# Branch B's transpositions and products spread over the tile, values two tiles behind the scores, and the third head's projections ahead of the token sums

## The chip, the core and the metric

One core of one Trainium2 chip. The time is the device time of one execution in microseconds (us), the median of several runs; the profile is of one more execution of the same program. Engines: PE does matmuls (and loads their weights, PEld), DVE is the vector engine, ACT the scalar engine, POOL is GpSimd, and SP issues nearly all DMAs. PSUM is the memory that PE writes to, in banks of 128 x 512 fp32; everything else lies in SBUF or in DRAM.

## The reference

A pre-norm encoder block on 1024 tokens of width 1024, with 16 meta tokens put in front (L = 1040). Two attention branches read the same normed input h; a SwiGLU feed-forward part follows.

```python
proj = h @ w_in                       # qa ka va | qb kb vb | ga gb
# A: 4 heads of 2 x 64 (q, k) and 128 (v), every token sees every token
attn = softmax(s1) - lam * softmax(s2)     # s = q k / 8 - slope * |dist|
y_a = rms_norm(attn @ va, subln) * (1 - lambda_init)
# B: 8 query heads of 64 in 2 groups, one key/value head per group;
# a block of 128 queries sees 16 meta tokens and three blocks of 128 keys
p = exp(s - m); y_b = (p / (sum(p) + exp(sink - m))) @ vb
merged = sigmoid(ga) * (y_a @ w_ba) + sigmoid(gb) * (y_b @ w_bb)
x = x + merged @ w_o
x = x + (silu(n @ w_gate) * (n @ w_up)) @ w_down     # n = rms_norm(x)
```

## The kernel before

All matmuls have fp32 accuracy. An operand is split in a high part and a low part (hi, lo), and a product is three matmuls: hi x hi, hi x lo, lo x hi. A split is two instructions: ACT copies to the high part, and DVE or POOL subtracts it from the source for the low part. So nearly every tile that PE writes, and every weight that it reads, goes through ACT and then DVE or POOL.

**Stages.** In order, with the microseconds of the profiled execution: norm and transposition of x and the first projections (to 73); branch B (73 to 232); token sums (232 to 286); products of a Strassen-like scheme that reads them, for the queries of A and six gates (286 to 366, `product_t`); branch A (366 to 676); then the output products and the feed-forward part, which the change doesn't touch.

**Projection steps.** `project_steps` makes a projection of 128 columns in chunks of tokens; one step is the three matmuls of one 128-row block of the contraction, so a chunk has eight steps, and at its end the result is evicted and sent to DRAM (`va_evac`, `k_consume`). The chunks are 384, 384 and 272 tokens wide for keys and values of A, 512 for gates and for the second group's queries of B. Weights are loaded (`w_c`), then split by ACT (L185) and POOL (L188) in `prep`, `W_BUFS` = 2 projections ahead.

**The order.** A scheduler orders the instructions of ACT, DVE, POOL and SP from a model of the time line. PE's order, from L585 (branch B) to the end of the products and again in branch A (L878 on), is the order in which the Python code issues matmuls. Generators hold the pieces of work, and strings of slots say which one gives its next piece.

**Branch B** has 16 tiles: two groups with eight blocks of queries each. `attend_b` (L315) is one tile. For each of the four query heads it makes a pair of score matmuls into a bank (tag "bs" of PSUM, two banks), and DVE adds the distance term, takes the running maximum and writes the scores to the tile `bs` (L332); then ACT makes four exponentials (L338), DVE the denominators, and POOL normalises the four rows (L344) and copies the 16 meta columns to `bmd` (L348). `values()` does the rest of the tile: for each of its three blocks of keys (two at the ends) and then the meta block, four transpositions into a bank (tag "bt", two banks, L364), ACT's copy (L366), DVE's low part (L368), and, when more than two transposed blocks stand in the list `trs`, the products of the oldest into the bank "by" (L358: two matmuls of 512 columns for a block of keys, one for the meta block). The last product is the meta block's. ACT and DVE add the two halves of the bank (L379, L380), and four DMAs store it.

The scores of the tiles 0 and 1 are made first, in the prologue. In the loop from L592 the tile n gives scores while tile n-1 gives values, seven projection steps in a tile, by

```python
SLOTS_B = "sgsgsgstgtgttgtttgt"    # s scores of n, t values of n-1, g a projection step
```

The steps come from `fill_b` (L566): 176 in all, for values and keys of the heads 0, 1 and 2 of A, with the second group's queries of B in four pieces between those of head 0. Before the loop `B_FIRST` = 8 steps are made and one more beside each of the six pieces of tile 0's values, after it `B_LAST` = 10 and six beside the last tile's. With 14 rounds of seven, 128 steps lie in branch B, and the 48 of the third head (h = 2) lie behind it.

**Token sums.** `token_sums` (L613) makes on DVE, for a quarter of the tokens, four sums of the high and low parts of hT (L620), four more sums and differences of those (L623 to L626), and splits of the results into `tops` (L627; L121 on ACT, L122 on DVE). It is called before steps 0, 8, 16 and 24 of the third head's 48 (L636). The products (`product_t`, matmuls L696) read `tops` for four of their seven terms.

**Branch A** has 32 tiles (four heads with eight blocks). For a tile `scores_a` makes six pairs of score matmuls (L791; DVE L794), an exponential per map (L799, ACT), a scaling (L802, POOL) and the combination of both maps (L805, DVE); `transpose_a` transposes nine blocks in three banks (L817, then L820 and L821 on ACT and DVE); `values_a` makes the products of two tiles at a time (L830), and after every fourth tile `normed_a` normalises the head's output. In the loop from L888 the tile n gives scores and tile n-2 its transpositions. The slots "g" fill in projection steps of the fourth head of A and of ten gates (`fill_steps`, L737), the slots "n" step the products of older tiles (`step_tail`). At a new head `load_a` (L761) fetches its queries, keys and values from DRAM into buffers that the last head's scores still read; there `fill(G_HEAD)`, ten steps, stands ahead of the tile's slots, and 33 (`G_FIRST`) at the first head. `HOLD` = 36 of the gate steps are kept for the tail, where the products of the last tiles are made with three steps after each piece (L918 to L921).

Of the kernel before, what the change touches and what calls it, by code (L numbers as in the profile page):

```python
# [20 lines left out]
P = 128  # L21
# [9 lines left out]
BG = 2  # L31
# [11 lines left out]
SLOTS = "stgstgstgsngsnsn"  # L43
SLOTS_LAST = "stgstgstsngsnsn"
N_MORE = 13
SLOTS_B = "sgsgsgstgtgttgtttgt"
S_BUFS = (2, 2)
AT_BUFS = 2
G_BUFS = 3
HOLD = 36  # L50
PAIRS = 3
HEADS_EARLY = 3
GT_BUFS = 4
WB_BUFS = 5
G_HEAD = 10
G_FIRST = 33

QK_BUFS = 3
# [1 line left out]
X_BUFS = 2  # L60
T_LAG = 2
V_AT = 2
B_FIRST = 8
B_LAST = 10
E_STEPS = 1
OP_BUFS = 8
RING_RAW = 5
# [12 lines left out]
def encoder_block(ctx: ExitStack, tc: tile.TileContext, x, meta, norm_mix, w_in, lq1, lk1, lq2, lk2,  # L80
# [190 lines left out]
    def flush_v():  # L271
        for g in turning_v:
            for _ in g:
                pass
# [2 lines left out]
    bpool, close_bpool = pool("bpool")  # L277
    kb = [bpool.tile([P, 2, NT, 144], F32R, name=f"kb{g}") for g in range(BG)]
    vb = [bpool.tile([P, 9, P], F32R, name=f"vb{g}") for g in range(BG)]
    mds = [bpool.tile([P, 4, P], F32, name=f"bmd{i}") for i in range(2)]  # L280
    for i in range(2):
        nc.gpsimd.memset(f32(vb[i])[:, 8, :], 0.0)
        nc.gpsimd.memset(mds[i], 0.0)

    def kb_consume(st, at, n):
        b0, nb = at // P, n // P
# [28 lines left out]
    def attend_b(g, t, finish):  # L315
        nm = f"{g}_{t}"
        b0, b1 = max(t - 1, 0), min(t + 2, NT)
        nb = b1 - b0
        W = nb * 144
        j0 = b0 - t + 1  # L320
        tb = tbx[:, j0:j0 + nb, :].rearrange("p j k -> p (j k)")
        st = bpool.tile([P, 4, 432], F32, tag="bs", name=f"bs_{nm}", bufs=2)
        mn = small.tile([P, 4], F32, tag="bmn", name=f"bmn_{nm}")
        dn = small.tile([P, 4], F32, tag="bdn", name=f"bdn_{nm}")
        es = small.tile([P, 4], F32, tag="bes", name=f"bes_{nm}")
        hs = slice(4 * g, 4 * g + 4)
        for r in range(4):
            ps = bank(psum1, "bs", f"bps_{nm}_{r}", 2)
            for v in range(2):
                nc.tensor.matmul(ps[:, :W], qb[:, r, t * P:(t + 1) * P],  # L330
                                 kb[g][:, v, b0:b1, :].rearrange("p b k -> p (b k)"), start=(v == 0), stop=(v == 1))
            nc.vector.tensor_tensor_reduce(st[:, r, :W], ps[:, :W], tb, 2.0 ** -(4 * g + r + 1), nsink[:, 4 * g + r:4 * g + r + 1],  # L332
                                           ALU.add, ALU.min, mn[:, r:r + 1])
            if r < 3:
                yield
        nc.vector.tensor_tensor(es, mn, sinkb[:, hs], ALU.add)
        for r in range(4):
            nc.scalar.activation(st[:, r, :W], st[:, r, :W], AF.Exp, bias=mn[:, r:r + 1], scale=-1.0,  # L338
                                 accum_out=dn[:, r:r + 1])
        nc.scalar.activation(es, es, AF.Exp)  # L340
        nc.vector.tensor_tensor(dn, dn, es, ALU.add)
        nc.vector.reciprocal(dn, dn)
        for r in range(4):
            nc.gpsimd.tensor_scalar(st[:, r, :W], st[:, r, :W], dn[:, r:r + 1], 1.0, ALU.mult, ALU.mult)  # L344

        md = mds[t % 2]
        own = (t - b0) * 144 + P
        nc.gpsimd.tensor_copy(md[:, :, 0:2 * NM].rearrange("p r (a k) -> p r a k", a=2),  # L348
                              st[:, :, own:own + NM].unsqueeze(2).broadcast_to([P, 4, 2, NM]))

        def values():
            py = bank(psum1, "by", f"bpy_{nm}", 1)
            blocks = [(k, P, (k - b0) * 144) for k in range(b0, b1)] + [(8, P, (t - b0) * 144 + P)]
            trs = []

            def products(k, kp, tr):
                for hl in range(2 if k < 8 else 1):
                    nc.tensor.matmul(py, vb[g][:kp, k, :], tr[:kp, hl].rearrange("p r t -> p (r t)"),  # L358
                                     start=(k == b0 and hl == 0), stop=(k == 8))

            for k, kp, o in blocks:
                pt = bank(psum1, "bt", f"bpt_{nm}_{k}", 2).rearrange("p (r t) -> p r t", r=4)
                for r in range(4):
                    nc.tensor.transpose(pt[:kp, r, :], st[:, r, o:o + P] if k < 8 else md[:, r], ident)  # L364
                tr = bpool.tile([P, 2, 4, P], F32R, tag="btr", name=f"btr_{nm}_{k}", bufs=4)
                nc.scalar.activation(tr[:kp, 0], pt[:kp], AF.Copy)  # L366
                lo = tr[:, 1] if k < 8 else tr[:NM, 0]
                nc.vector.tensor_tensor(lo, pt[:lo.shape[0]], f32(tr[:lo.shape[0], 0]), ALU.subtract)  # L368
                trs.append((k, kp, tr))
                yield  # L370
                if len(trs) > 2:
                    products(*trs.pop(0))
                    yield
            while len(trs) > 1:
                products(*trs.pop(0))
                yield
            products(*trs.pop(0))
            y1 = bpool.tile([64, 512], F32, tag="by1", name=f"by1_{nm}", bufs=2)
            nc.scalar.copy(y1, py[64:128])  # L379
            nc.vector.tensor_tensor(y1, py[0:64], y1, ALU.add)  # L380
            for jj in range(2):
                for par in range(2):
                    r = 2 * jj + par
                    nc.sync.dma_start(yb_d[2 * g + jj][64 * par:64 * par + 64, t * P:(t + 1) * P],
                                      y1[:, r * P:(r + 1) * P])
            yield
        finish.append(values())
# [18 lines left out]
    def norm_x(t):  # L406
        parts = P if t < NT else NM
        i = len(done)
        done.append(t)
        p, tag, bufs = (stage, "vt", 1) if i % 3 == 2 else (bpool, "bs", 2)  # L410
        xns[t] = normed(p, xts.pop(t)[:parts], parts, gmix, f"a{t}", tag=tag, bufs=bufs)

    def turn_x(t):
# [146 lines left out]
    def v_steps_a(h):  # L560
        return v_steps(C_VA + h * P, f"va{h}", va_evac(h))
# [4 lines left out]
    def fill_b():  # L566
        def prepared(steps):
            ensure(1)
            yield from with_turns(steps)
            ensure(W_BUFS - 1)  # L570

        for h in range(HEADS_EARLY):
            yield from prepared(v_steps_a(h))
            if not h:
                for jj in range(2):
                    yield from prepared(qb_steps(1, qb, jj, Q_CHUNKS[:1]))
            yield from prepared(k_steps_a(h))
            if not h:
                for jj in range(2):
                    yield from prepared(qb_steps(1, qb, jj, Q_CHUNKS[1:]))  # L580


    order_pe = tc.manual_schedule(engines={mybir.EngineType.PE})
    order_pe.__enter__()
    more = fill_b()  # L585
    for _ in range(B_FIRST):
        next(more)
    for _ in finish.pop(0):
        next(more)
    for n in range(2, BG * NT):  # L590
        scoring, values = attend_b(*divmod(n, NT), finish), finish.pop(0)
        for what in SLOTS_B:  # L592
            next({"s": scoring, "t": values, "g": more}[what], None)
        for _ in chain(scoring, values):
            pass
    for _ in range(B_LAST):
        next(more)
    for _ in finish.pop(0):
        next(more)
    close_bpool()  # L600


# [30 lines left out]
        return (hT_hi, hT_lo)[b][:, 4 * kh + c, th * 512:th * 512 + 512]  # L633


    for i, _ in enumerate(more):  # L636
        if i % 8 == 0 and i < 32:
            token_sums(i // 8)
    flush_v()
    close_psum1()  # L640
    psum_t, close_psum_t = pool("psum_t", space=PSUM)
    psum1 = psum_t
# [217 lines left out]
    def fill(n):  # L860
        while n > 0 and n_gates[0] > 0:
            n, n_gates[0] = n - 1, n_gates[0] - 1
            next(gates, None)
# [24 lines left out]
    for n in range(AH * NT + T_LAG):  # L888
        scoring, turning = iter(()), iter(())
        if n < AH * NT:  # L890
            h, t = divmod(n, NT)
            if t == 0:
                ld = load_a(h)
                fill(G_HEAD if h else G_FIRST)
            if t % 2 == 0:
                at_ = apool.tile([P, 9, 2, 256], F32R, tag="at", name=f"at{h}_{t}", bufs=AT_BUFS)
            s = [None, None]
            tiles.append((h, t, s, at_, ld[2]))
            scoring = scores_a(h, t, ld, s)
        if n >= T_LAG:  # L900
            turning = turn(tiles[n - T_LAG])
        for what in SLOTS if n < N_MORE else SLOTS_LAST:
            if what == "s":
                next(scoring, None)
            elif what == "t":
                next(turning, None)
            elif what == "n":
                step_tail()
            else:
                fill(1)  # L910
        for _ in scoring:
            pass
        for _ in turning:
            pass
        if n >= T_LAG and tiles[n - T_LAG][1] % 2:
            tail.append(later(tiles[n - T_LAG]))
    n_gates[0] += HOLD
# [610 lines left out]
```

## Time and profile before

| | |
|---|---|
| runs | 1501.68 us median of 3 (1497.37 to 1503.5) |
| profiled execution | 1496.41 us |
| its span in the trace | 1494.5 us |
| granted clock of PE, mean | 0.993 |
| DMA | 193.13 MB, mean 129 GB/s |

The span runs from the first to the last record; the profiled execution's own time is 1.9 us longer. Busy time is the union of an engine's instructions. A row of the timeline gives start, duration, engine, line of the kernel, instruction, output <- inputs and shape; a number in brackets at its end is the time for which the engine stood idle before it, with what ended the wait. A row of the waits gives the waiting instruction, the one that released it, the sum of the waits in us, their count and the longest. Names have their buffer numbers left out: `bpt` is a bank for the transpositions of B, `btr` the transposed tile with both parts, `bpy` the bank of its products; `aps`, `apt` and `apy` are the same for A, `ak` its keys, `as` its scores; `pp_va`, `pp_ka`, `pp_qb`, `pp_g` are banks of projections. A clock share of 1.00 is the full granted clock of PE.

### The profile page before, as it was taken

Reading aid. Unit: us, or ns where it says so; the run is one execution under the profiler, and the core shown is the slowest. Engines: PE = TensorE matmul, PEld = TensorE weight load, DVE = VectorE, ACT = ScalarE, POOL = GpSimd, SP = SyncE. Lnnn points to the kernel's source line nnn. Section 1 sums busy time; section 2 is a strip of 40 time slices with the busy share of each in tenths; the row PEclk is TensorE's granted clock in tenths of the full one; section 3 lists DMA queues with packets and bytes.
Section 4 is the critical chain, followed back from the end, with each engine's and each line's share of the span. In section 5 each row is a group of like instructions: output and inputs, shape, how many; then the busy total and the mean of one; then the engine's idle time right before and its main releaser. Section 6 shows DMA issues by size and latency. Waiting matters only on the chain.

```text
span 1494.5 us, 21017 instructions
## 1 busy us (share of the span) xinstructions
PE 1446.2 (97%) x7315; PEld 1229.3 (82%) x7315; DVE 896.1 (60%) x1635; ACT 689.9 (46%) x1296; POOL 563.0 (38%) x555
## 2 busy tenths in 40 slices
PE   8999998899899999999999999999999999999997
PEld 7977788688789888978888878888888888888886
DVE  6467768721668787814442586745555554778567
ACT  6366663432555565625532463333333333444444
POOL 4244431544222322313763315544554553000344
PEclk9999999999999999999999999999999999999999
DMA  8423314433633414137653244333333333864433
GB/s 233 90 81 98 99 44 146 124 124 114 181 94 99 142 65 128 51 124 244 210 189 113 77 128 155 110 102 106 106 106 106 106 106 106 300 230 133 133 122 141
DMA packets 154203, 193.13 MB, mean 129 GB/s; under 512 B 16288, under 2 KB 98656, under 8 KB 154096
## 3 DMA queue, kind: packets, MB, share of 16 engines
q1 hardware_dynamic: 154096, 191.78, 40.6%
q8 instruction: 58, 0.95, 0.3%
q14 instruction: 49, 0.40, 0.1%
HBM read 131.24 MB, written 53.94 MB: 124 GB/s over the span
## 4 chain that ended last, share of the span: by engine, by line
PE 74%; DVE 7%; DMA 6%; issue 5%; POOL 3%; ACT 3%; SPq 1%; POOLq 0%; DVEq 0%; ACTq 0%
PE pg L1309 27%; PE pd L1403 8%; PE po L1075 6%; PE pt L696 5%; PE pp_g L215 5%; PE ppa L734 4%; PE aps L791 3%; PE apy L830 3%; POOL oa L122 3%; PE pp_qb L215 2%; DMA ak<-ka_d 2%; PE apt L817 2%; PE bpy L358 1%; PE pp_ka L215 1%; PE pp_va L215 1%
## 5 line engine op out<-in xcount | busy, mean ns | idle before, releaser
L1309 PE MATMUL pg<-t,wop 128*128 128x512 f32 x1056 | 243.0, 389 | 1.6 <-DVE wop L122 1.6
L1309 PEld LDWEIGHTS pg<-t,wop 128*128 128x128 f32 x1056 | 198.0, 188 | 43.4 <-DVE wop L122 2.0
L122 POOL TENSOR_TENSOR wop<-wf,wop 128x512 fp32r<-128x512 f32 x118 | 157.5, 1336 | 156.5 <-ACT wop L121 145.5
L1403 PE MATMUL pd<-ob,oa 128*128 128x512 f32 x924 | 210.0, 389 | 0.4 <-POOL oa L122 0.4
L1403 PEld LDWEIGHTS pd<-ob,oa 128*128 128x128 f32 x924 | 173.3, 188 | 37.0 <-POOL oa L122 0.8
L1309 PE MATMUL pg<-b,wop 128*128 128x512 f32 x792 | 183.2, 389 | 0.0
L1309 PEld LDWEIGHTS pg<-b,wop 128*128 128x128 f32 x792 | 148.5, 188 | 30.8
L121 ACT ACTIVATE wop<-wf 128x512 fp32r<-128x512 f32 x128 | 80.3, 632 | 82.3 <-PE pg L1309 50.4
L122 POOL TENSOR_TENSOR oa<-ra,oa 128x512 fp32r<-128x512 f32 x33 | 44.0, 1335 | 170.1 <-ACT oa L121 168.7
L799 ACT ACTIVATE as<-as,amn 128x1040 f32<-128x1040 f32 x64 | 74.5, 1164 | 64.9 <-DVE amn L794 50.8
L121 ACT ACTIVATE oa<-ra 128x512 fp32r<-128x512 f32 x77 | 48.7, 632 | 106.6 <-PE pd L1403 50.2
L791 PE MATMUL aps<-ak,aq 128*128 128x352 f32 (+1 forms) x384 | 92.4, 332 | 3.4 <-DMA ak<-ka_d 2.8
L188 POOL TENSOR_TENSOR wl_c<-w_c,wh_c 128x512 fp32r<-128x512 f32 x48 | 61.9, 1311 | 84.7 <-ACT wh_c L185 74.6
L1075 PE MATMUL po<-woh,mT 128*128 128x512 f32 x384 | 88.6, 390 | 0.0
L1075 PEld LDWEIGHTS po<-woh,mT 128*128 128x128 f32 x384 | 71.7, 188 | 14.7
L1133 DVE TENSOR_TENSOR s<-wf,wf 128x512 f32<-128x512 f32 x22 | 18.2, 829 | 108.1 <-DMA wf<-in_w_ff_up_dram 53.1
L791 PEld LDWEIGHTS aps<-ak,aq 128*128 128x128 f32 x384 | 66.8, 191 | 15.7 <-issue 4.4
L122 POOL TENSOR_TENSOR wop_t<-wt,wop_t 128x512 fp32r<-128x512 f32 x30 | 46.5, 1554 | 60.8 <-ACT wop_t L121 59.3
L802 POOL TENSOR_SCALAR as<-as,adn,neglam 128x1040 f32<-128x1040 f32 x32 | 38.8, 1213 | 80.6 <-DVE adn L800 71.7
L215 PE MATMUL pp_g<-hT_hi,wh_c 128*128 128x512 f32 x160 | 68.9, 431 | 0.0
L344 POOL TENSOR_SCALAR bs<-bs,bdn 128x432 f32<-128x432 f32 (+1 forms) x64 | 36.9, 596 | 75.3 <-ACT btr L366 55.7
L215 PE MATMUL pp_g<-hT_hi,wl_c 128*128 128x512 f32 x160 | 63.3, 395 | 0.0
(279 smaller groups left out, 3175.2 us busy)
## 6 DMA issues: line engine op xcount, KB each, us to landing
ra<-aop SPq DMA_DIRECT2D x77, 256.0 KB, 2.6
w_c<-in_w_in_dram SPq DMA_DIRECT2D x25, 512.0 KB, 4.2
wf<-in_w_ff_gate_dram SPq DMA_DIRECT2D x24, 512.0 KB, 3.6
wf<-in_w_ff_up_dram SPq DMA_DIRECT2D x24, 512.0 KB, 3.6
aop<-as SPq DMA_DIRECT2D x44, 256.0 KB, 2.1
aop<-c SPq DMA_DIRECT2D x33, 256.0 KB, 2.0
gt<-g_d SPq DMA_DIRECT2D x32, 256.0 KB, 3.2
wt<-in_w_in_dram SPq DMA_DIRECT2D x10, 512.0 KB, 5.4
```

Source lines behind the costliest of these rows:

```text
L121: nc.scalar.activation(hi, src, AF.Copy)
L122: lo_eng.tensor_tensor(lo, src, f32(hi), ALU.subtract)
L188: (lo_eng or nc.gpsimd).tensor_tensor(wl[:, c], w[:, c], f32(wh[:, c]), ALU.subtract)
L215: nc.tensor.matmul(ps[:, :n], a[:, c, :], b[:, c, at:at + n], start=(c == 0 and i == 0), stop=(c == DC - 1 and i == 2))
L696: nc.tensor.matmul(ps, op[:, 4 * a + c], moving(p, c, b), start=(p in (1, 2, 5) and c == 0 and n == 0), stop=(p in (4, 2, 3) and c == 3 an ...
L734: nc.tensor.matmul(ps, w[:, a, j, :], src(j, b, tk), start=(j == 0 and n == 0), stop=(j == 3 and n == 2))
L791: nc.tensor.matmul(ps[:, :n], qs[m][:, t * P:(t + 1) * P], ks[m][:, vv, k0:k0 + n], start=(vv == 0), stop=(vv == 1))
L799: nc.scalar.activation(s[m][:, 0:L], s[m][:, 0:L], AF.Exp, bias=low, scale=-1.0, accum_out=dn[:, m:m + 1])
L830: nc.tensor.matmul(py[:, cols], v[:kp, a, k, :], at_[:kp, k, b, :], start=(k == 0 and j == 0), stop=(k == 8))
L1075: nc.tensor.matmul(ps, mT[:, c, a, t * P:(t + 1) * P], wos[q, c][:, b], start=(c == 0 and n == 0), stop=(c == DC - 1 and n == 2))
L1309: nc.tensor.matmul(ps, op[:, x, c, :], b[:, y, c, :], start=(p in (1, 2, 5) and c == 0 and n == 0), stop=(p in (4, 2, 3) and c == 3 and n ...
L1403: nc.tensor.matmul(ps[u], oa[:, a, u * P:(u + 1) * P], ob[:, b, :], start=(p in (1, 2, 5) and j == 0 and k == 0), stop=(p in (2, 3, 4) and ...
```

## The change

In branch B the values lag two tiles behind the scores instead of one. The slot string has a new letter, "y", which takes the last piece of the values of the tile before (its last product, and the eviction), so that this piece comes at the head of the next tile. There are eight projection steps in a tile instead of seven, with at most two slots of one kind in a row, and products are made as soon as more than one transposed block is in the list, instead of two. Scores have three buffers instead of two, and so has the meta block's tile `bmd`. The loop runs two rounds longer, which have no scores, and takes over what stood ahead of and behind it: six steps stand ahead of it, none behind. With 6 + 16 x 8 = 134 steps, six of the third head's now lie in B.

The other 42 are issued in one piece, and then, after the last transpositions of that head's values and keys, all four token sums (on engines other than PE the scheduler may place them earlier).

In branch A the three later heads make seven steps instead of ten at their start, in two pieces: four, then all transpositions of tile n-2, a step of the products, and three. The tiles 1 and 2 have three steps more at their end. `HOLD` is 39 instead of 36, so three steps more are kept for the tail.

`fill_b` is written in another order of lines that gives the same steps.

```diff
-SLOTS_B = "sgsgsgstgtgttgtttgt"
-HOLD = 36
+HOLD = 39
-G_HEAD = 10
+G_HEAD = 7
-B_FIRST = 8
-B_LAST = 10
+S_BUFS_B = 3
+B_FIRST = 6
+SLOTS_B = "ysgtgsgtgtsgtgtsgtgt"
...
-    mds = [bpool.tile([P, 4, P], F32, name=f"bmd{i}") for i in range(2)]
+    mds = [bpool.tile([P, 4, P], F32, name=f"bmd{i}") for i in range(3)]
...
-        st = bpool.tile([P, 4, 432], F32, tag="bs", name=f"bs_{nm}", bufs=2)
+        st = bpool.tile([P, 4, 432], F32, tag="bs", name=f"bs_{nm}", bufs=S_BUFS_B)
...
-        md = mds[t % 2]
+        md = mds[(g * NT + t) % 3]
...
                 yield
-                if len(trs) > 2:
+                if len(trs) > 1:
                     products(*trs.pop(0))
                     yield
...
-    more = fill_b()
+    more, last = fill_b(), iter(())
     for _ in range(B_FIRST):
         next(more)
-    for _ in finish.pop(0):
-        next(more)
-    for n in range(2, BG * NT):
-        scoring, values = attend_b(*divmod(n, NT), finish), finish.pop(0)
+    for n in range(2, BG * NT + 2):
+        scoring = attend_b(*divmod(n, NT), finish) if n < BG * NT else iter(())
+        values = finish.pop(0)
         for what in SLOTS_B:
-            next({"s": scoring, "t": values, "g": more}[what], None)
-        for _ in chain(scoring, values):
+            next({"s": scoring, "t": values, "y": last, "g": more}[what], None)
+        for _ in chain(last, scoring):
             pass
-    for _ in range(B_LAST):
-        next(more)
-    for _ in finish.pop(0):
-        next(more)
+        last = values
+    for _ in last:
+        pass
     close_bpool()
...
-    for i, _ in enumerate(more):
-        if i % 8 == 0 and i < 32:
-            token_sums(i // 8)
+    for _ in more:
+        pass
     flush_v()
+    for u in range(4):
+        token_sums(u)
     close_psum1()
...
             if t == 0:
                 ld = load_a(h)
-                fill(G_HEAD if h else G_FIRST)
+                if not h:
+                    fill(G_FIRST)
...
+        if n in (NT, 2 * NT, 3 * NT):
+
+            fill(G_HEAD - 3)
+            for _ in turning:
+                pass
+            step_tail()
+            fill(3)
         for what in SLOTS if n < N_MORE else SLOTS_LAST:
...
         for _ in turning:
             pass
+        if n in (1, 2):
+            fill(3)
```

More of the change, by code (lines that the diff above doesn't have):

```diff
@@ L279, in encoder_block @@
     vb = [bpool.tile([P, 9, P], F32R, name=f"vb{g}") for g in range(BG)]
-    mds = [bpool.tile([P, 4, P], F32, name=f"bmd{i}") for i in range(2)]
+    mds = [bpool.tile([P, 4, P], F32, name=f"bmd{i}") for i in range(3)]
     for i in range(2):
         nc.gpsimd.memset(f32(vb[i])[:, 8, :], 0.0)
-        nc.gpsimd.memset(mds[i], 0.0)
+    for md in mds:
+        nc.gpsimd.memset(md, 0.0)
     def kb_consume(st, at, n):
@@ L409, in norm_x @@
         done.append(t)
-        p, tag, bufs = (stage, "vt", 1) if i % 3 == 2 else (bpool, "bs", 2)
+        p, tag, bufs = (stage, "vt", 1) if i % 3 == 2 else (bpool, "bs", S_BUFS_B)
         xns[t] = normed(p, xts.pop(t)[:parts], parts, gmix, f"a{t}", tag=tag, bufs=bufs)
@@ L570, in prepared @@
             ensure(W_BUFS - 1)
-        for h in range(HEADS_EARLY):
+        yield from prepared(v_steps_a(0))
+        for jj in range(2):
+            yield from prepared(qb_steps(1, qb, jj, Q_CHUNKS[:1]))
+        yield from prepared(k_steps_a(0))
+        for jj in range(2):
+            yield from prepared(qb_steps(1, qb, jj, Q_CHUNKS[1:]))
+        for h in range(1, HEADS_EARLY):
             yield from prepared(v_steps_a(h))
-            if not h:
-                for jj in range(2):
-                    yield from prepared(qb_steps(1, qb, jj, Q_CHUNKS[:1]))
             yield from prepared(k_steps_a(h))
-            if not h:
-                for jj in range(2):
-                    yield from prepared(qb_steps(1, qb, jj, Q_CHUNKS[1:]))
     order_pe = tc.manual_schedule(engines={mybir.EngineType.PE})
     order_pe.__enter__()
-    more = fill_b()
+    more, last = fill_b(), iter(())
     for _ in range(B_FIRST):
         next(more)
-    for _ in finish.pop(0):
-        next(more)
-    for n in range(2, BG * NT):
-        scoring, values = attend_b(*divmod(n, NT), finish), finish.pop(0)
+    for n in range(2, BG * NT + 2):
+        scoring = attend_b(*divmod(n, NT), finish) if n < BG * NT else iter(())
+        values = finish.pop(0)
         for what in SLOTS_B:
-            next({"s": scoring, "t": values, "g": more}[what], None)
-        for _ in chain(scoring, values):
-            pass
-    for _ in range(B_LAST):
-        next(more)
-    for _ in finish.pop(0):
-        next(more)
+            next({"s": scoring, "t": values, "y": last, "g": more}[what], None)
+        for _ in chain(last, scoring):
+            pass
+        last = values
+    for _ in last:
+        pass
     close_bpool()
```

## Prediction

> **What bounds the kernel now.** I read the page first, then the busy time of each stage, then in each stage what the matmul engine (PE) waits for.
>
> ```profile
> span 1494.5 us, 21017 instructions
> PE 1446.2 (97%) x7315; PEld 1229.3 (82%) x7315; DVE 896.1 (60%) x1635; ACT 689.9 (46%) x1296; POOL 563.0 (38%) x555
> ```
>
> PE is busy for 97% of the span, and the change neither adds nor removes a matmul. So it can only move PE's stops: 48.3 us by the page. The stages, in the columns window, its length, busy time of PE, PE's weight loads, DVE, ACT and POOL, clock share, DMA share:
>
> ```profile
> 73.00:232.00 159.00, 148.50 (x859) 127.95 (x860) 106.33 (x263) 101.16 (x244) 61.58 (x96) 1.00 0.31 86
> 232.00:286.00 54.00, 45.41 (x231) 40.27 (x229) 50.49 (x71) 22.38 (x42) 21.57 (x10) 0.94 0.34 101
> 286.00:366.00 80.00, 80.00 (x349) 65.52 (x350) 20.22 (x30) 28.05 (x48) 37.28 (x29) 1.00 0.41 126
> 366.00:412.00 46.00, 39.99 (x235) 37.98 (x235) 25.80 (x76) 20.71 (x36) 13.35 (x16) 0.93 0.71 190
> 412.00:638.00 226.00, 220.97 (x1398) 199.70 (x1396) 177.32 (x519) 128.33 (x234) 65.39 (x80) 1.00 0.31 97
> ```
>
> The first row is branch B, the second the token sums (DVE busy 50.5 of 54: DVE bounds it), the third has no idle time, the fourth is the start of branch A, the fifth the rest of A. The change touches all but the third. In B, PE's waits are:
>
> ```profile
> PE bpt L364 <- DVE btr L368: 7.6, 8, 1.9
> PE bpy L358 <- DVE btr L368: 1.5, 5, 0.6
> PE bpt L364 <- DVE bdn L341: 0.5, 1, 0.5
> ```
>
> That is 10.5 us idle by the first row of the windows, nearly all of it transpositions that wait for a PSUM bank to be emptied. The end of one tile (PE's rows in time, then DVE's subtraction between them) shows what the idle column leaves out:
>
> ```profile
> 219.49 0.60 PE L364 MATMUL bpt<-ident,bmd 128*128 128x128 f32 x4
> 219.85 1.17 PE L358 MATMUL bpy<-btr,vb 128*128 128x512 f32 x4
> 220.85 0.34 PE L215 MATMUL pp_ka<-hT_hi,wh_c 128*128 128x384 f32 x1
> 221.03 0.34 PE L215 MATMUL pp_ka<-hT_lo,wh_c 128*128 128x384 f32 x1
> 221.20 0.34 PE L215 MATMUL pp_ka<-hT_hi,wl_c 128*128 128x384 f32 x1
> 221.55 0.50 PE L358 MATMUL bpy<-btr,vb 128*128 128x512 f32 x1
> 221.89 0.34 PE L215 MATMUL pp_ka<-hT_hi,wh_c 128*128 128x384 f32 x1
> ```
>
> ```profile
> 220.82 0.68 DVE L368 TENSOR_TENSOR btr<-bpt,btr 16x512 fp32r<-16x512 f32 x1 [0.74 <-ACT btr L366]
> ```
>
> A 384-wide matmul is listed with 0.34 us, but the next starts 0.17 to 0.18 after it, so a stop is about 0.17 longer than its idle time. The last product of the tile (221.55) could start at about 221.38, and it loses 0.17 of which no idle shows. Fourteen listed waits and sixteen last products, with 0.17 to 0.28 each, bring the 10.5 us to about 17.
>
> **Branch B, the new order.** The changed kernel's instruction order, engine by engine, shows one projection step or pair of score matmuls between any two pieces of a tile's transpositions and products, and the transpositions read scores of two tiles before. So the 7.6 and 0.5 us of waits for banks and for the softmax should go, but for about 1.2 at the first tile, where the copies still queue behind the first exponentials. What is late next is the last product. Its operand is the fourth transposition (the meta block), and the chain is in the rows: from the transposition's first matmul (219.49) through ACT's copy and DVE's subtraction to the product (221.55) are 2.06 us. Before, four products and a step stood between. Now there are one step and two products, and the last product is the next tile's first entry. Arrival: transpositions 0.36 (219.49 to 219.85), a step of three 384-wide matmuls 0.53, two products 0.50 (half of 219.85 to 220.85): 1.39, so a stop of 0.67, and 0.1 at the restart (221.55 to 221.89 in place of 0.25, a quarter of the four products before). With a step of 512-wide matmuls (0.70, by its width) it is 0.6, with a 272-wide one (0.38) 0.9. In the order this stands in twelve inner tiles (six, two and four of these steps): 4.6 + 1.2 + 3.6 = 9.4 us. The four tiles at a branch's edge put a score pair and a second step in between and don't wait. In three tiles ACT's last exponential stands ahead of the copy, about 0.3 each. Sum: 9.4 + 0.9 + 1.2 = 11.5 in place of 17, **5.5 us won**. Bounds: the twelve stops cost nothing if the chain overlaps better (17 won), or 1.4 us more each, if every copy came as late as the longest listed wait (1.9) says (11 lost).
>
> Of the third head's projections five 384-wide steps and one 272-wide more now stand ahead of B's last product: 5 x 0.53 + 0.38 = 3.0 us. It comes 2.5 us earlier.
>
> **Token sums.** These rows carry the stage: DVE's groups of sums (last columns: mean ns, idle before), its order at the start, POOL's weight splits, and two of PE's stops:
>
> ```profile
> L620 DVE TENSOR_TENSOR f<-hT_hi,hT_lo 128x512 f32<-128x512 f32 x16 | 12.8, 834 | 0.0
> ...
> L666 DVE TENSOR_TENSOR s<-wt,wt 128x512 f32<-128x512 f32 x3 | 3.1, 1048 | 1.2 <-DMA wt<-in_w_in_dram 1.2
> ...
> L624 DVE TENSOR_TENSOR f<-f,f 128x512 f32<-128x512 f32 x4 | 2.7, 682 | 0.0
> ```
>
> ```profile
> 232.96 0.68 DVE L380 TENSOR_TENSOR by<-bpy,by 64x512 f32<-64x512 f32 x1 [1.58 <-ACT by L379]
> ...
> 234.70 6.42 DVE L620 TENSOR_TENSOR f<-hT_hi,hT_lo 128x512 f32<-128x512 f32 x8
> ```
>
> ```profile
> 233.97 2.99 POOL L188 TENSOR_TENSOR wl_c<-w_c,wh_c 128x512 fp32r<-128x512 f32 x2 [13.26 <-ACT wh_c L185]
> ...
> 272.47 5.40 POOL L122 TENSOR_TENSOR wop_t<-wt,wop_t 128x512 fp32r<-128x512 f32 x1 [4.71 <-ACT wop_t L121]
> ```
>
> ```profile
> 275.60 0.50 PE L696 MATMUL pt<-tops,wop_t 128*128 128x512 f32 x1 [1.77 <-DVE tops L122]
> 277.93 6.90 PE L696 MATMUL pt<-tops,wop_t 128*128 128x512 f32 x22 [1.83 <-POOL wop_t L122]
> ```
>
> The sums start when B's last eviction leaves DVE, and then DVE runs without a stop. The order of the sums on DVE is nearly the same after the change, and their count is. So PE's third-head projections hide behind DVE, with six steps fewer: PE only waits longer at 275.60. What counts is when DVE starts and how long it takes. It starts 2.5 us earlier with B, and 1.1 more because the first sum then follows B's last eviction at once (233.64 instead of 234.70; an eviction of keys no longer stands between). It takes less by the 1.2 us wait (the third head's weights are split earlier, so the buffer of the load is free earlier) and about 1.0 because the split at 233.97 no longer falls beside the first sums: 834 against 682 ns is what the sums pay beside POOL. The stage's end comes **5.8 us earlier**. Bounds: 0, if POOL's starved split (5.40 us) decides alone, to 8.
>
> **Start of A.** Three steps go behind the scores of the tiles 1 and 2.
>
> ```profile
> 394.71 0.83 PE L817 MATMUL apt<-ident,as 128*128 128x128 f32 x4 [2.38 <-DVE as L805]
> ...
> 408.91 1.09 PE L817 MATMUL apt<-ident,as 128*128 128x128 f32 x4 [2.85 <-DVE adn L800]
> ```
>
> ```profile
> 391.70:395.00 3.30, 0.92 (x8) 0.63 (x7) 2.62 (x7) 1.63 (x3) 0.28 (x2) 1.00 0.79 259
> 395.10:398.40 3.30, 3.30 (x17) 3.16 (x16) 2.05 (x8) 2.34 (x4) 1.01 (x1) 0.50 0.23 72
> ```
>
> After a window with 2.38 idle the clock is granted at 0.50 for 3.3 us, which costs half of that, 1.65. Two waits and two such stretches: 2.38 + 2.85 + 3.3 = 8.5 us. The first three steps (272-wide, 1.1 us) cover part of the first wait, and the 1.3 left should not lower the clock. The second three (512-wide, 2.0 us, taken as three times 0.69) come before the next tile's scores, and in the changed order the combination that the second wait is for stands further ahead on ACT and DVE: this wait should go. **7.0 us won**; bounds 4 (both waits shorter, one stretch of half clock stays) to 8.5.
>
> The Trainium skill (TensorE: Matmul & The Clock Gate, Why this matters for your kernels) advises against gaps over about 3 us. Here a gap of 2.38 was enough; by the page the half clock would have another cause, and the sum would keep its 3.3 us (a rival below).
>
> **Head boundaries and tail.** At the three later heads ten steps become seven.
>
> ```profile
> 502.00:517.00 15.00, 14.16 (x74) 11.59 (x72) 8.70 (x26) 7.23 (x14) 5.17 (x6) 1.00 0.89 265
> ```
>
> ```profile
> 517.41 0.40 PE L791 MATMUL aps<-ak,aq 128*128 128x352 f32 x1 [0.89 <-DMA ak<-ka_d]
> ```
>
> ```profile
> 507.59 9.69 DMA ak<-ka_d
> ```
>
> The keys' transfer starts when the last head's scores release the buffer and lands at a time that PE doesn't move. PE waits for it already, and the transpositions now put ahead stood ahead of this wait before. So three steps fewer are 2.0 us more of waiting, 6.2 at three heads. The transfers are busy for 0.89 of this stretch at 265 GB/s. In the changed order of SP's queue a gate's store (256 KB, 1.0 us at that rate) no longer stands between the keys' loads at two of the three heads; I take half of it back: **5.2 us lost**, bounds 3 to 9, the upper one with the clock lowered twice. The other stores and weight loads of the moved steps keep their places beside fewer transfers. The tail gets three steps more (HOLD). They cover nothing there, since ACT evicts the last gate before it splits yb, as before; it is work only moved.
>
> **Sum:** -5.8 - 7.0 + 5.2 = -7.6 us on the profiled execution of 1496.41 (span 1494.5 and 1.9 around it): 1488.8. The median shown is 5.3 above that, so I predict 1494.0. The bound of the chances is 0.5% (7.5 us, 1494.2), about what a measurement can tell from no change.
>
> **Rivals.**
> - *Slower:* the copy of the meta block queues in ACT behind exponentials in every inner tile. Against it: in nine of twelve tiles the order has it ahead of the last one. For it: the longest listed wait of this kind is 1.9. If a last product costs over 2.0 us in place of 0.8, 15 us or more are lost against the forecast and the kernel ends slower than before; with 2.6, at 1510. Chance 0.18.
> - *The boundaries take more:* no transfer is earlier (1.0), and PE's three waits of 3 us lower the clock twice (2 x 1.65): 1498. Chance 0.09.
> - *The sums end when they did:* POOL's starved split decides (the row at 277.93 names it), and B's gain is given back before 286 us: 1500. Chance 0.07.
> - *The edit doesn't spread the work:* excluded for PE, whose order is written out by hand.
> - *Better:* the last products wait half as long (4.7), and the boundaries lose only 3 (2.2): 1487. Chance 0.22.
> - *The clock isn't lowered by gaps under 3 us,* as the page just named has it, and the half clock has a cause that the change leaves: its 3.3 us stay, 1497. The two windows speak against it. Chance 0.02.
>
> **How the numbers follow.** The forecast has 0.42, its own range 1490 to 1498, about half of it on each side of the bound. Faster: 0.21 + 0.22 = 0.43. Within 0.5%: 0.21 + 0.09 + 0.07 + 0.02 = 0.39. Slower: 0.18. The range 1484 to 1506 holds all but the worse half of the slower case and the edge of the better one; 3 us of it are the scatter of the runs shown.
>
> **What would show it.** In the changed profile: waits of transpositions in B near 1 us in sum, a last product of each inner tile that starts 2.06 after its transposition; the first L620 near 231; no idle at the second transposition of A and no half clock near 395 and 409; about 2 to 3 us at each keys' wait. The forecast is wrong if the meta block's copy starts more than 0.5 us after its transposition, or if DVE's sums still end near 280.

## The result, and the profile after

The changed kernel takes 1494.72 us in the median of ten runs (1492.09 to 1497.67), the kernel before 1499.47 in ten (1496.0 to 1503.5). The ratio is 0.9967, with a 95% interval of 0.9951 to 0.9982: 4.9 us faster, between 2.7 and 7.3. The profiled execution of the changed kernel took 1494.14 us, which is 2.3 less than that of before.

The page of the changed kernel, its span and busy times:

```profile
span 1492.4 us, 21014 instructions
PE 1443.1 (97%) x7315; PEld 1228.8 (82%) x7315; DVE 892.0 (60%) x1635; ACT 687.9 (46%) x1296; POOL 562.7 (38%) x556
```

The stages by busy time (same columns as in the prediction; the windows are put at the same points of the work, so they lie earlier):

```profile
73.00:229.30 156.30, 148.10 (x876) 131.20 (x876) 103.27 (x262) 101.12 (x242) 64.26 (x98) 1.00 0.32 88
229.30:280.50 51.20, 43.11 (x212) 37.44 (x211) 48.16 (x70) 20.80 (x40) 18.66 (x8) 0.90 0.39 115
280.50:360.50 80.00, 80.00 (x350) 65.53 (x351) 21.17 (x30) 28.03 (x48) 37.26 (x29) 1.00 0.40 119
360.50:406.50 46.00, 43.03 (x263) 40.32 (x262) 26.12 (x77) 21.22 (x38) 13.40 (x16) 1.00 0.75 196
406.50:633.00 226.50, 215.43 (x1360) 194.12 (x1358) 178.54 (x518) 126.63 (x233) 65.12 (x80) 0.99 0.31 96
```

PE's idle time in B went from 10.5 to 8.2 us with more work in the stage (876 matmuls instead of 859), and at the start of A from 6.0 to 3.0. In the last row it rose from 5.0 (220.97 of 226) to 11.1 (215.43 of 226.5). PE's waits name the new stops:

```profile
PE aps L792 <- DMA ak<-ka_d: 8.5, 8, 1.7
PE bpy L359 <- DVE btr L369: 7.1, 13, 0.8
PE pt L697 <- DVE tops L122: 3.3, 1, 3.3
PE pt L697 <- DVE qk_stage L233: 3.0, 1, 3.0
...
PE apt L818 <- DVE as L806: 2.5, 2, 1.7
```

The first row is PE's scores that wait for a new head's keys: 2.8 us before, 8.5 now. The second is the last product of a tile, which takes the place of the transpositions' waits (7.6 us before). Starts of the same instruction in both traces show where the time came from; the difference is running, so each step between two rows is what one part of the kernel won or lost:

| start of | before | after | difference |
|---|---|---|---|
| first score of B | 66.65 | 65.95 | -0.70 |
| last product of B | 231.91 | 228.96 | -2.96 |
| first score of A, head 0 | 382.58 | 377.05 | -5.53 |
| tile 7 of A | 433.08 | 425.68 | -7.40 |
| tile 10, behind the first boundary | 461.93 | 456.25 | -5.68 |
| tile 15 | 499.21 | 493.52 | -5.69 |
| tile 18, behind the second | 527.72 | 521.14 | -6.58 |
| tile 23 | 563.80 | 557.22 | -6.59 |
| tile 26, behind the third | 591.71 | 585.36 | -6.35 |
| tile 29 | 612.24 | 607.18 | -5.06 |
| first output product | 761.55 | 758.73 | -2.82 |
| end of the span | 1494.54 | 1492.37 | -2.18 |

The prologue's 0.70 is counted apart. The first score of B stands between 65.95 and 67.85 in the twelve traces, later where PE runs at half clock (0.50) for 6.83 us near 15 us instead of 3.41. That none of it is the change's isn't shown: the third buffer of the scores (`S_BUFS_B`) also serves the normed rows of x in the prologue, which have the same tag, and the six traces with it and the shorter stretch have this score 0.2 to 0.7 us earlier than the profile shown in front, which has the shorter stretch too. In A the moved steps have to be counted: a step of three 512-wide matmuls is 0.69 us. Up to tile 7 the changed kernel has made six steps more (4.1 us), so it stopped 1.9 + 4.1 = **6.0 us less** (1.9 is what it gained in the table from head 0's first score to tile 7). At each boundary it makes three less (2.1 us): it stopped 1.7 + 2.1 = 3.8, -0.9 + 2.1 = 1.2 and 0.2 + 2.1 = 2.3 longer, in sum **7.3 us more**. Another 1.3 are lost between the tiles 26 and 29. The three steps that HOLD adds to the tail are 2.1 of the 2.2 lost there.

### The profile page after: what moved, and what is told of

The parts are those of the page before. It is cut to its first block, busy times and chain, and to the rows that moved or that the text cites. A ratio compares the mean times of both kernels' runs of the same rounds, so it can differ in the third digit from the quotient of the medians.

```text
span 1492.4 us, 21014 instructions
## 1 busy us (share of the span) xinstructions
PE 1443.1 (97%) x7315; PEld 1228.8 (82%) x7315; DVE 892.0 (60%) x1635; ACT 687.9 (46%) x1296; POOL 562.7 (38%) x556
## 4 chain that ended last, share of the span: by engine, by line
PE 77%; DMA 7%; DVE 5%; issue 4%; POOL 4%; ACT 2%; SPq 1%; POOLq 0%; ACTq 0%; DVEq 0%
PE pg L1320 28%; PE pd L1414 8%; PE pt L697 6%; PE po L1086 6%; PE pp_g L215 5%; PE aps L792 4%; PE ppa L735 4%; PE apy L831 3%; DMA ak<-ka_d 3%; POOL oa L122 3%; PE pp_qb L215 3%; PE apt L818 2%; PE bpt L365 1%; PE pp_ka L215 1%; PE pp_va L215 1%
## 5 line engine op out<-in xcount | busy, mean ns | idle before, releaser
L1086 PEld LDWEIGHTS po<-woh,mT 128*128 128x128 f32 x384 | 71.7, 188 | 14.7
```

Source lines behind the costliest of these rows:

```text
L1086: nc.tensor.matmul(ps, mT[:, c, a, t * P:(t + 1) * P], wos[q, c][:, b], start=(c == 0 and n == 0), stop=(c == DC - 1 and n == 2))
```

## The experiments

Theory: the forecast's mechanisms hold, and branch B's part and the three steps at the start of A each win, but the shortened boundaries lose more than the start wins. Rival: the two profiled executions are single draws, and branch A's part is worth the 1.8 us that the forecast gave it.

**Branch B's part alone**, then **branch A's part alone**, against the kernel before.

```diff
# e1, against the changed kernel
-HOLD = 39
+HOLD = 36
-G_HEAD = 7
+G_HEAD = 10
-                if not h:
-                    fill(G_FIRST)
+                fill(G_HEAD if h else G_FIRST)
-        if n in (NT, 2 * NT, 3 * NT):
-            fill(G_HEAD - 3)
...
-            fill(3)
-        if n in (1, 2):
-            fill(3)
# e2, against the kernel before: the same lines of branch A the other way round, nothing in branch B
```

> Branch B and the order of the token sums as changed, branch A as before. By the trace of the changed kernel (first score matmul of A 4.8 us earlier beyond what the prologue gave, first output product only 3.1 us earlier) this part wins 4.8 and branch A's part then loses 2.5: against the kernel before 4.8 us faster in the profile's landmarks, about 2.5 us faster than the changed kernel. By the forecast's terms it wins 5.8 against before, and is 1.8 us slower than the changed kernel, because branch A's part is worth 1.8.

> Branch A as changed (three steps behind the scores of tiles 1 and 2, seven in two pieces at the heads, 39 kept for the tail), branch B and the token sums as before. By the trace of the changed kernel: start 6 us better, boundaries 8 us worse, 0 to 1 us worse elsewhere: 2 to 3 us slower than before. By the forecast's terms (7.0 won, 5.2 lost): 1.8 us faster than before.

Branch B's part alone: 1490.64, ratio 0.9944 (0.9930 to 0.9957), 8.4 us faster. Branch A's part alone: 1501.64, ratio 1.0014 (1.0004 to 1.0025), 2.1 us slower. The rival falls: branch A's part costs time. Branch B's part wins more by the medians than either theory expected, while its profile gives the expected size (first score of A 4.04 us earlier although its prologue was 0.93 later, so 5.0). The end of the next part comes back to this.

**The start of A without the shorter boundaries.** The boundaries are as before, the two times three steps stay, and the six steps are taken from the tail.

```diff
# e3, against the changed kernel
-HOLD = 39
+HOLD = 30
-G_HEAD = 7
+G_HEAD = 10
-                if not h:
-                    fill(G_FIRST)
+                fill(G_HEAD if h else G_FIRST)
-        if n in (NT, 2 * NT, 3 * NT):
-            fill(G_HEAD - 3)
...
-            fill(3)
```

> As changed, but the heads' boundaries as before (ten steps in one piece), the two times three steps at the start of A kept, and HOLD 30, so that the six steps come out of the tail. If the start's 6 us and the boundaries' 8 us are separate and the tail's steps cover nothing: boundaries lose nothing, start keeps its win, some 8 us faster than the changed kernel, 13 faster than before; the waits for the keys back at about 0.5 to 1.6 us a head. If the tail's steps did cover something, up to 4.1 us (six steps of 0.69) of it come back as waits in the tail: 4 us faster than the changed kernel.

1488.86, ratio 0.9932 (0.9920 to 0.9944): 10.2 faster than before, 5.3 faster than the changed kernel, between the two cases. The boundaries lose nothing: from 7.4 us earlier than before at tile 7 it comes to 10.8 at tile 26, with as many steps as before, so PE stops 3.4 us less there. The last keys land 14.2, 12.2 and 12.8 us after a head's first load is issued, in the kernel before 14.6, 14.7 and 14.1; the six steps put other gate stores and weight loads beside them, and which of these makes the difference isn't shown. Of the waits for keys, 0.7 us is left, at head 0:

```profile
PE ppa L735 <- ACT yb L121: 3.4, 1, 3.4
...
PE aps L792 <- DMA ak<-ka_d: 0.7, 1, 0.7
```

The first row shows what the tail's steps are for. With 30 instead of 36, PE waits 3.4 us for the split of yb in place of 1.25, and two windows of half clock follow (661.40 to 668.23). From the last score to the first output product it takes 129.5 us where the kernel before takes 128.5, although six steps (4.1 us) are gone: they did cover something.

The chain of work shows a boundary with seven steps (the first one of the changed kernel) and one with ten (the second one of e3):

```profile
431.98 0.42 PE aps L792 x2
...
433.27 0.45 SPq L771
433.72 0.04 issue
433.76 10.19 DMA ak<-ka_d
443.96 0.14 issue
444.09 0.40 PE aps L792
```

```profile
497.20 0.42 PE aps L792 x2
497.61 6.95 PE pp_g L215 x30
504.56 0.33 PE aps L792 x2
```

With seven steps the chain leaves PE with the last score of the old head, goes through SP's issues and the 10.19 us of the last keys' transfer, and comes back to PE when it has landed. With ten it stays on PE.

**The order at the boundary.** As e3, but the ten steps in the changed kernel's two pieces.

```diff
# e6, against the changed kernel
-HOLD = 39
+HOLD = 30
-G_HEAD = 7
+G_HEAD = 10
```

> As e3_start_hold30, but with ten steps at a head in the changed kernel's two pieces (seven, the transpositions of tile n-2 and a step of the products, three). Only the order at the boundaries differs. If the changed kernel's loss there (8.0 us with seven steps) is that of nine steps missing: within 1.5 us of e3, and waits for the keys of at most 0.5 us a head. If it is the transpositions, put ahead of the new head's scores instead of between them: the scores that wait for the second keys have nothing between them, 1 to 1.7 us of waits a head and 3 to 5 us slower than e3.

1488.37, ratio 0.9941 (0.9925 to 0.9957), as e3 within the intervals. So by the medians the number of steps decides, and not the pieces. That the pieces cost nothing isn't shown, since the six runs lie apart: four from 1486.1 to 1488.4, two at 1493.0 and 1493.3, and the profiled execution is one of the two. There the keys at the second boundary come 11.5 us after their issue instead of 8.0 in e3, PE waits 1.32 and 1.18, and a window of half clock follows:

```profile
499.46 11.52 DMA ak<-ka_d
510.99 0.14 issue
511.12 0.40 PE aps L792
```

The transfers issued up to the keys' landing are the same in both kernels; in e6's execution they moved 254, 244 and 285 GB/s from 495 to 507 us, in e3's 279, 304 and 304. Why the rate differed stays open. Counted as in the table above, the three boundaries of this execution lose 2.2 us against the kernel before, 1.7 of it the half clock; in the four profiled executions with ten steps in one piece (e3, e5, e7, e8) they win 1.1 to 3.3. The waits are those that the second case of the expectation names, in one execution of the slower kind.

**The last product later.** It stands behind a score pair and a projection step of the next tile.

```diff
# e4, against the changed kernel
-SLOTS_B = "ysgtgsgtgtsgtgtsgtgt"
+SLOTS_B = "sgytgsgtgtsgtgtsgtgt"
```

> As changed, but the last product of a tile is put behind the first score pair and the first projection step of the next tile instead of ahead of them. If the last product waits only for the 2.06 us chain of the meta block (copy and subtraction): a score pair (0.39) and a step (0.4 to 0.7) cover the 0.5 to 0.8 that it waits now, the 7.1 us of these waits go, B ends 7 to 9 us earlier and, since DVE starts the token sums that much earlier, the end is some 7 us earlier than in the changed kernel. If the waits only move (the transposition or the next product then waits for ACT or DVE instead, because these are late by themselves): B ends within 2 us of the changed kernel's.

1487.52, ratio 0.9929 (0.9916 to 0.9941): 10.6 faster than before, 5.7 faster than the changed kernel by the ratios. In its profile the last product of B starts at 222.26, 6.7 us earlier than in the changed kernel (228.96), and the first score of A is 5.9 earlier (371.12). Of the thirteen waits of last products only short ones are left (0.34 and 0.18 us in the inner tiles). So the waits were those of the 2.06 us chain, and it could be hidden. At the third boundary this execution lost more than the changed kernel's:

```profile
PE aps L792 <- DMA ak<-ka_d: 6.7, 6, 1.7
...
PE aps L792 <- issue: 1.7, 1, 1.7
```

Three waits of 1.57 to 1.65 us there and two windows of half clock (565.33 to 572.16) bring it from 17.4 us ahead of the kernel before, at tile 23, to 11.2 at tile 25. The shortened boundary is in e4 as in the changed kernel.

**The tail's steps, and both improvements together.**

```diff
# e5, against e3; e8, against e7
-HOLD = 30
+HOLD = 36
# e7, against e3
-SLOTS_B = "ysgtgsgtgtsgtgtsgtgt"
+SLOTS_B = "sgytgsgtgtsgtgtsgtgt"
```

> As e3_start_hold30 (heads' boundaries as before, three steps behind tiles 1 and 2), but HOLD 36: the six steps come out of the slots of the last tiles instead of the tail. In e3 the tail stopped 3.36 us in place of 1.25 for yb's split and had 6.8 us of half clock, some 5.4 us of stops for 4.1 us of steps less. If PE's slots in the last tiles cover nothing: the last score matmul 4.1 us earlier than in e3, the tail 1.0 longer minus, in all 5 us faster than e3 (15 faster than before). If each of them covers its whole length: the last score matmul as in e3 and the tail as before, 1 us faster or slower than e3.

> e3_start_hold30 and e4_y_later together (last product behind a score pair and a step, three steps behind tiles 1 and 2, boundaries of ten steps, HOLD 30). If the two are separate, their wins against the changed kernel add: 5.9 + 7.2 by the medians, 17 us faster than before, near 1482. If the end of B sets when transfers collide at a boundary, as the waits of e4 at the third boundary suggest (1.57, 1.65 and 1.63 us), up to 4 us of it are lost.

> e7_y_start30 with HOLD 36. What e5 gives against e3 should be given here too, 0 to 5 us: 1477 to 1482 if the two are separate.

e5: 1486.11, ratio 0.9918 (0.9906 to 0.9930); about 2 us better than e3 by the ratios, between its two cases, with intervals that overlap. Its tail has the kernel before's 1.25 us wait for yb again. The tiles 30 and 31 have no steps left in e5, and there it gains 3.3 us on e3, where six steps are 4.1: in the last tiles they cover little. e7: 1479.90, ratio 0.9875 (0.9862 to 0.9888); e8: 1479.03, ratio 0.9873 (0.9856 to 0.9890). The wins add: e7 is 18.7 us faster than before, where 17 was expected. HOLD makes no difference that these runs can tell between e7 and e8. Both beat the kernel before and the changed one.

**The kernel before, again.** For the difference between medians and profiles:

> The kernel before, one more profile. The changed kernel is 4.8 us faster by the medians and 2.2 by the two profiled executions, and branch B's part alone 8.5 by the medians and 4.7 by the profile. If a part of B's price before is not in the profile shown: its longest wait in B (1.95 us near 113) stands at the edge of lowering the clock and does so in some executions, as it did with the same code in e2 (0.50 from 116.81 on for 3.41 us): half clock near 117 and the end some 1.7 us later, or none and the end near 1494.5, by chance of where the 3.41 us windows fall. If the profile shown was low for another reason: no half clock in B, and a time near 1499.

> The kernel before once more, a second draw for the same question: half clock near 117 with a later end, or none.

1498.92 and 1500.32 us, spans 1497.1 and 1498.5. No half clock in B in either, so the first case of the expectation isn't what sets these two apart from the profile shown in front. Both lose 1.6 us at another place by the same mechanism: their stop before the last transpositions of A (2.10 us at 636 in the profile shown in front) is followed by a window of half clock at 638.49 and 639.23. In the execution shown in front it isn't. So the same stop costs or doesn't cost 1.7 us more. Behind the prologue e9 has this window of half clock on top of those of the execution shown in front. e10 has as many as that one in all, because the one near 409 isn't there; its head 0 waits 2.41 us for keys instead of 0.72. The profile on which the sum was made was thus the fastest of three draws.

## Why the prediction was right or wrong

The forecast was 1494.0, and the median came to 1494.72. It rested on 7.6 us less than before; measured are 4.9 (2.7 to 7.3) by the ratio, and 2.3 between the profiled executions. The rest of the agreement is luck: the forecast started from a median of three runs, 1501.68, and ten runs gave 1499.47, so 2.7 us too much won were set off by 2.2 us too high a start. At 0.9967 the change stays within the 0.5% that the forecast took as no change, to which it gave 0.39, against 0.43 for faster. Two slips in its sums don't touch this: the parts of the start of A add up to 7.2, not 7.0, and 2.6 us for each of twelve last products would end near 1516, not 1510. The case that happened is one between the forecast and the rival of the boundaries.

**Branch B: right.** The last product of B was to start 2.5 us earlier and starts 2.3 earlier (2.96 less the prologue's 0.70). The chain is the one named; PE's rows at the end of a tile, and ACT's and DVE's between them:

```profile
193.36 0.60 PE L365 MATMUL bpt<-ident,bmd 128*128 128x128 f32 x4
...
194.18 0.63 PE L359 MATMUL bpy<-btr,vb 128*128 128x512 f32 x2
195.43 0.50 PE L359 MATMUL bpy<-btr,vb 128*128 128x512 f32 x1 [0.62 <-DVE btr L369]
```

```profile
194.06 0.60 ACT L367 ACTIVATE btr<-bpt 128x512 fp32r<-128x512 f32 x1 [0.80 <-PE bpt L365]
```

```profile
194.69 0.68 DVE L369 TENSOR_TENSOR btr<-bpt,btr 16x512 fp32r<-16x512 f32 x1 [0.56 <-ACT btr L367]
```

From 193.36 to 195.43 are 2.07 us, where 2.06 was taken. Twelve of the thirteen listed waits (7.1 us) are those of the inner tiles that had been counted with 9.4: 6.9 listed and some 0.2 each that no idle shows. The slower rival (the copy queues behind exponentials in every tile) needed 2.0 us of stop a tile; the largest is 0.80. ACT starts the copy at most 0.5 us after the transposition ends.

**Token sums: right in kind, 1.0 too much.** The stage's end (first score of A) was to come 5.8 earlier and came 4.8 earlier without the prologue's part. DVE began 3.3 earlier (3.6 forecast). The first eight sums went faster without POOL's split beside them, 4.89 instead of 6.42: 1.5 where 1.0 was forecast. What failed is the 1.2 us won because "the buffer of the load is free earlier". The load is earlier: the rows of DVE that wait for it start at 238.93 instead of 244.76, 5.8 us earlier. But DVE reaches that point 6.2 earlier (237.41 instead of 243.60), so its wait didn't go.

```profile
230.72 4.89 DVE L620 TENSOR_TENSOR f<-hT_hi,hT_lo 128x512 f32<-128x512 f32 x8
...
238.93 0.69 DVE L667 TENSOR_TENSOR s<-wt,wt 128x512 f32<-128x512 f32 x1 [1.52 <-DMA wt<-in_w_in_dram]
```

It is 1.52 instead of 1.16, in place of the nothing in the forecast: 1.5 us mis-sized. The three sizes, 3.3 + 1.5 - 0.4, make 4.4 of the 4.8; where the other 0.4 comes from isn't shown. The rival in which the sums end when they did, because POOL's starved split decides, didn't occur; that split took 4.20 us here and PE waited for DVE's `tops` instead (3.3 us). Half clock in the stage went from two windows to three, which the sum didn't have either. Behind them PE no longer has a stop of 1.07 us that it had there before, so what the third window cost isn't shown.

**Start of A: right, 1.0 too much.** 6.0 of 7.0. Both half-clock stretches are gone (1.00 in the stage's row). Of the first wait 0.73 is left where 1.3 was forecast, and the second is gone. But three stops stand there that the sum didn't have: head 0's keys make PE wait 1.27 instead of 0.72, a transposition of the fourth head's values waits 0.41 for an eviction, and a score pair 0.55 for a bank's copy.

**Head boundaries: the step that was mis-sized.** 7.3 us in place of 5.2, within the bounds of 3 to 9. "The keys' transfer starts when the last head's scores release the buffer and lands at a time that PE doesn't move" holds, as the chain above shows; that it is the steps, e3 shows, and e6 by its median. The 1.0 taken back for the gate's store can't be seen in this execution: the last keys land 14.9, 14.1 and 14.6 us after a head's first load is issued, in sum as late as before (14.6, 14.7 and 14.1). And the first boundary lowered the clock, which the forecast had only in a rival and in its upper bound:

```profile
441.70:445.10 3.40, 1.40 (x8) 1.18 (x9) 0.57 (x3) 1.08 (x2) 2.03 (x2) 1.00 0.35 128
445.20:448.50 3.30, 3.30 (x14) 3.10 (x14) 1.18 (x4) 0.00 (x0) 1.21 (x1) 0.50 0.56 165
```

A window with 2.0 us idle, and the next at 0.50: 1.7 us. Without it the boundaries lost 5.6, between the 5.2 of the forecast and the 6.2 of the bare steps. The same shortened boundaries stand in e2 and e4. Counted in the same way they lose 4.5 us in e2, with no half clock there, and 8.3 in e4, with two windows of it (3.4). So without half clock the three executions lose 4.5, 5.6 and 4.9, which is the forecast's size, and the term that the sum put at nothing is the half clock: it came in two of the three.

**Left out.** Between the tiles 26 and 29 the changed kernel loses 1.3 us that the sum didn't have. It comes with the six steps at the start, which shift every later gate step: e2 to e8, which all have them, lose 1.2 to 1.3 between the same tiles, and e1, which doesn't, loses nothing. Which eviction then holds which instruction isn't shown; two of the stops there are for A's normalisation (`apf`, 0.4) and a copy's low part (0.35).

**Tail: right for the steps added, not in general.** "They cover nothing there" fits the three steps added (2.1 of 2.2 us came on top), but not the six taken away in e3, where the wait for yb grew from 1.25 to 3.36.

Why branch B's part wins 8.4 us by the medians (6.4 to 10.5 by the interval) and 5.0 by its profile is not settled as a whole. The draws account for the size: the profiled execution of before is 2.8 us under the median of the runs beside e1 (1496.41 against 1499.2), and e1's is 1.0 above its own (1491.65 against 1490.64). Of what differs between executions one piece is seen: the kernel before has a stop of 1.94 us in B (at 113 to 115 us). In e2, with the same code in B, it was followed by half clock, in the three other executions with that code not. It is not in the changed B at all.

## What to carry to other kernels

Filler work that is moved out of a stretch comes back there as waiting, for most of its length (4.5 to 5.6 of 6.2 us here), if a transfer sets the end of that stretch, and costs more if the longer stop lowers the clock (7.3 and 8.3 us). Find the landing that PE can't move before taking cover away from it, and count all places, here three boundaries against one start. A dependent chain of copy and subtraction (2.06 us here) can be taken from a matmul's path by issuing the matmul two pieces of other work later, in the next tile: that was worth another 5.7 us. And before a sum is made on one profiled execution, a second one shows which of its stops lower the clock by chance.

## What the runs showed of the hardware that was not expected

The granted clock is lowered by what falls into one window of 3.41 us, and the windows lie differently in each execution. Within each of the twelve traces all stretches of half clock start whole multiples of 3.41 us apart, so the windows can be counted off from them through the whole trace. Cut in this way between 50 and 1470 us, the twelve traces have 39 windows at full clock in which PE is idle for more than 1.90 us, and all 39 are followed by half clock; of 34 windows with 1.50 to 1.85 us idle two are, and of 4867 with less also two. The kernel before, in the two windows around its 1.95 us stop in B, and then e2 with the same stop:

```profile
111.75:115.15 3.40, 1.77 (x10) 1.19 (x8) 2.62 (x4) 2.26 (x5) 2.69 (x3) 1.00 0.26 60
115.15:118.57 3.42, 3.10 (x18) 2.73 (x19) 1.45 (x3) 0.97 (x2) 2.51 (x5) 1.00 0.76 193
```

```profile
113.40:116.80 3.40, 1.46 (x9) 1.00 (x8) 3.21 (x5) 1.33 (x3) 3.40 (x4) 1.00 0.41 95
116.82:120.22 3.40, 3.40 (x13) 2.64 (x11) 0.68 (x1) 0.60 (x1) 1.57 (x4) 0.50 0.81 213
```

In the first the stop is cut by the window's end: 1.63 us idle, then 0.32, and the clock stays at 1.00. In e2 all of it lies in one window, 1.94 idle, and the next is granted 0.50. The Trainium skill (TensorE: Matmul & The Clock Gate, Why this matters for your kernels) warns of PE-idle gaps over about 3 us. Here 1.94 us within one window was enough, and the measurement decides. So a stop of about 2 us has a price that changes by 1.7 us from execution to execution.
